# Two weight pairs of gate and up taken straight in each FFN instead of three

## The chip, the cores and the metric

The kernel runs on one core of a Trainium2 chip. The metric is the device time of one execution in microseconds (us), lower is better. The core has five engines with their own instruction queues: TensorE (PE in the profile, with its weight loads as PEld), VectorE (DVE), ScalarE (ACT), GpSimd (POOL) and SyncE (SP), which here only issues loads. Each executes its own queue in order and waits on semaphores for the others.

## The reference

A trunk of two layers over 512 tokens of width 1024. Each layer is a half-step FFN, a mixer (neighbourhood attention beside gated linear attention) and a second half-step FFN; a last norm follows. The change is in the FFN, which runs four times:

```python
D_MODEL = 1024; SEQ = 512; DEPTH = 2; D_FF = 2816

def rmsnorm(x, g):
    y = x * lax.rsqrt(jnp.mean(x * x, axis=-1, keepdims=True) + EPS)
    return y * g

def swiglu(h, w_gate, w_up, w_down):
    return (jax.nn.silu(h @ w_gate) * (h @ w_up)) @ w_down

# in hybrid_layer, twice per layer, with the mixer between:
x = x + 0.5 * swiglu(rmsnorm(x, ffn1_norm), ffn1_wg, ffn1_wu, ffn1_wd)
x = x + concat(neighbourhood attention, gated linear attention) @ w_out
x = x + 0.5 * swiglu(rmsnorm(x, ffn2_norm), ffn2_wg, ffn2_wu, ffn2_wd)
```

## The kernel before

The activations lie transposed, eight chunks of 128 features by 512 tokens (`xt`). Every fp32 operand is split into a high and a low half: ScalarE makes the high one by a copy (`split`, L149), VectorE the low one by a subtraction (L150), and each product is three matmuls, high x high, high x low, low x high (`mm3`, L169 to L171). So every matrix costs work on all three engines.

The 2816 hidden columns of gate and up are cut into 11 pairs of 2 x 128 columns, and the pairs into groups of 4, 4 and 3 (`GROUPS`); after each group its part of the down matrix follows (`down`), delayed into the next group's first pair. A pair's gate matrix and up matrix (1024 x 256 each, 1 MB) are multiplied in one of two ways.

- Straight (`direct_pairs`, `dmat`): from `XD`, the split of raw x times the norm's gain. It needs no norm factor; that is multiplied in afterwards (`evac`, L392 to L395). Two outputs by 8 chunks by 3 are 48 matmuls of 512 columns for a matrix. The weights come in four loads of 256 KB on ScalarE's queue (`dload`).
- By the block product (`smat`, `gate_up`): the weights and the normalised x are cut 2 x 2 and multiplied with seven products instead of eight. 7 x 4 x 3 are 84 matmuls of 256 columns for a matrix. The weights come in one 1 MB load on SyncE's queue; VectorE forms four sums of weight blocks (L269 to L272) and ScalarE and VectorE split seven blocks. The right-hand side is `XC`, which `prep_pair` makes from `xt` and the norm factor, two chunks at a time in four calls (L179 to L187 on VectorE, then its splits). All pairs of the FFN use the same `XC`.

At the start of an FFN the norm factor of a row (`stage_row`) is not there yet: the squares were summed while the last chunks of x were made, one matmul with ones adds them over partitions (L232), and ScalarE and VectorE take the inverse root (L242 to L250). The straight pairs stand in the first group, so that TensorE has work meanwhile: pair 0 (results in PSUM tiles `F_mm`), pair 1 (gate in `F_sc`, up in `F_tp` and `F_o`), pair 2 (`F_mm` again). `prep_pair` for chunks 0 to 5 is written between pair 1's gate and up matrices, that for the last two after the evacuation of pair 0; pairs 1 and 2 are evacuated after that. The block product then begins with pair 3.

The order of instructions on each engine isn't the order of the program text: a scheduler arranges them by its own cost estimates, over buffers of a fixed number (`wh` and `wl` six each, four PSUM tiles `mm`, two `sc`, one `tp` and `o`, five for the weight sums). It is fixed before the kernel runs. In the names of tiles, `F_xd` (`I_xd`, `OP_xd` in the first FFN and behind a mixer) are parts of `XD`, `F_xc` of `XC`, `F_y` its unsplit chunks, `F_wh` and `F_wl` the halves of a weight block, `F_wraw` a load, `F_ws` the weight sums, `F_r` the norm factor, `F_hid` the split hidden activations and `F_o` an evacuated result, or the PSUM tile "o".

Of the kernel before, what the change touches and what calls it, by code (L numbers as in the profile page):

```python
# [53 lines left out]
COLS = {"q": 0, "k": 512, "v": 1024, "gq": 1536, "gk": 1792, "gv": 2048, "gr": 2560}  # L54
TAGS = {'sl': 12, 'g0': 8, 'g1': 8, 'na': 6, 'ws': 5}
NPR = 12
NDF = 3
OPT = 2.56
OUTT = 8.24
GOTT = ('g0', 'g1')  # L60
# [3 lines left out]
def trunk_kernel(ctx, tc, xin, wgu, wdn, win, wcode, wgate, wout, vec, rpbt,  # L64
# [111 lines left out]
    def prep_pair(i, stage):  # L176
        s = st["s"]
        ya, yb = sl("y"), sl("y")
        V.scalar_tensor_tensor(ya, xt[:, 2 * i, :], gvec(stage, 2 * i), s, ALU.mult, ALU.mult)  # L179
        V.scalar_tensor_tensor(yb, xt[:, 2 * i + 1, :], gvec(stage, 2 * i + 1), s, ALU.mult, ALU.mult)  # L180
        ta, tb = sl("y"), sl("y")
        b11, b12, b21, b22 = ya[:, :H2], ya[:, H2:], yb[:, :H2], yb[:, H2:]
        t1, t2, t3, t4 = ta[:, :H2], ta[:, H2:], tb[:, :H2], tb[:, H2:]
        V.tensor_tensor(t1, b12, b11, op=ALU.subtract)
        V.tensor_tensor(t2, b22, t1, op=ALU.subtract)
        V.tensor_tensor(t3, b22, b12, op=ALU.subtract)
        V.tensor_tensor(t4, b21, t2, op=ALU.subtract)  # L187
        tag = ("na", "na", "g0", "g1")[i]
        h0 = sl("xc", F32R, tag)
        split(b11, h0[:, :H2], h0[:, H2:])  # L190
        parts = [(h0[:, :H2], h0[:, H2:])]
        if i < 2:
            xg = gp_.tile([P, 4, T], F32R, tag="ga", name=nm("xc"))
        for j, src in enumerate((yb, ta, tb)):
            if i < 2 and j < 2:
                h, l = xg[:, 2 * j, :], xg[:, 2 * j + 1, :]
            else:
                h, l = sl("xc", F32R, tag), sl("xc", F32R, tag)
            split(src, h, l)
            parts += [(h[:, :H2], l[:, :H2]), (h[:, H2:], l[:, H2:])]  # L200
        XC[i] = dict(zip(("b11", "b21", "b22", "t1", "t2", "t3", "t4"), parts))
# [128 lines left out]
    def dmat(*args):  # L330
        pss = []
        run(dmat_steps(pss, *args))
        return pss
# [24 lines left out]
    def ffn(l, which):  # L358
# [3 lines left out]
        stage = 3 * l + 2 * which  # L362
        fp = [NDF]

# [21 lines left out]
        def direct_pairs(hid):  # L386

            def evac(bg, bu):
                r = st["s"]
                for ps, pu in zip(bg, bu):  # L390
                    g, u = sl("o1"), sl("o2")
                    V.tensor_tensor(g, ps, r, op=ALU.mult)  # L392
                    S.activation(g, g, AF.Silu)
                    V.tensor_tensor(u, pu, r, op=ALU.mult)
                    V.tensor_tensor(u, u, g, op=ALU.mult)  # L395
                    add_hid(hid, u)

            raw, ws = st.pop("dpre", (None, None))
            b00 = dmat(wgu[idx, 0, 0], ("mm", "mm"), raw, ws)
            if stage == 0:  # L400
                nc.scalar.dma_start(con, onesid)
                for c in range(KD):
                    square(c)
            stage_row()
            b01 = dmat(wgu[idx, 0, 1], ("mm", "mm"))
            b10 = dmat(wgu[idx, 1, 0], ("sc", "sc"))
            for i in range(3):
                prep_pair(i, stage)
            b11 = dmat(wgu[idx, 1, 1], ("tp", "o"))
            evac(b00, b01)  # L410
            prep_pair(3, stage)
            if NDF == 3:
                b20 = dmat(wgu[idx, 2, 0], ("mm", "mm"))
            evac(b10, b11)
            if NDF == 3:
                evac(b20, dmat(wgu[idx, 2, 1], ("mm", "mm")))
# [45 lines left out]
        for g, n in enumerate(GROUPS):  # L462
            hid = []
            if g == 0:
                direct_pairs(hid)
                n -= NDF
                if stage == 0:
# [683 lines left out]
```

## Time and profile before

| | |
|---|---|
| three runs | 1954.86, 1954.99, 1955.47 us |
| the profiled execution | 1957.23 us, of which the trace spans 1955.5 |
| mean granted TensorE clock | 0.991 |
| PE busy | 1924.7 us, 12490 instructions |
| DVE busy | 1416.9 us, 2705 instructions |
| ACT busy | 1020.1 us, 1959 instructions |

All times below are from the one profiled execution and count from the start of its span. An instruction's duration holds the time until its result is out; the next one of the same engine may start earlier, so what a run of instructions costs is read from start to start. Matmul ends are modelled and overlap: a 512-column matmul is shown with 0.39 us, and the next starts 0.23 after it. A value in brackets behind a row is the time for which the engine stood idle before it, and what ended that.

### The profile page before, as it was taken

The page shows a single profiled execution, that of the slowest core. Times are in us where ns is not written, and L with a number is a line of the kernel's source. Part 1 is how long each engine was busy: PE and PEld are TensorE (multiplying, and loading weights), DVE is VectorE, ACT ScalarE, POOL GpSimd, SP SyncE. Part 2 cuts the span into 40 slices and gives each one's busy share as a digit, 9 for nine tenths or more (in the row PEclk, how much of TensorE's full clock was granted, in tenths as well). Part 3 has the DMA queues.
Part 4 walks back from the last instruction along what each step waited for, and adds up shares of the span by engine and source line. Part 5 has one row for each costly group of instructions (what it writes and reads, how often), then busy time and mean ns, then how long its engine had stood idle before and what let it go on. Part 6 is the DMA issues. An engine that isn't in the chain of part 4 may idle for free.

```text
span 1955.5 us, 32220 instructions
## 1 busy us (share of the span) xinstructions
PE 1924.7 (98%) x12490; PEld 1687.4 (86%) x12490; DVE 1416.9 (72%) x2705; ACT 1020.1 (52%) x1959; POOL 17.4 (1%) x36
## 2 busy tenths in 40 slices
PE   8999999999998999999999999999999999999997
PEld 7889989888777898999889899988887778999896
DVE  6958768676558875967788596776764689679585
ACT  5535536465564553644555364455654655546364
POOL 0000000000000000000000000000000000000000
PEclk9999999999999999999999999999999899999999
DMA  4333223322202332332223333232221033233322
GB/s 154 112 108 108 89 106 124 110 67 98 66 31 85 102 108 89 106 108 103 83 98 106 108 109 107 88 119 96 96 86 55 21 120 107 89 107 109 108 76 76
DMA packets 58249, 187.78 MB, mean 96 GB/s; under 512 B 6640, under 2 KB 13296, under 8 KB 45808
## 3 DMA queue, kind: packets, MB, share of 16 engines
q1 hardware_dynamic: 29904, 132.07, 19.8%
q10 hardware_dynamic: 25632, 45.27, 7.0%
q0 software_dynamic: 2560, 8.39, 1.3%
q8 instruction: 98, 1.61, 0.3%
q14 instruction: 55, 0.45, 0.1%
HBM read 183.60 MB, written 2.10 MB: 95 GB/s over the span
## 4 chain that ended last, share of the span: by engine, by line
PE 97%; DVE 1%; DMA 1%; ACT 1%; issue 0%; DVEq 0%; ACTq 0%
PE F_mm L169 14%; PE F_mm L171 14%; PE F_mm L170 14%; PE F_sc L169 9%; PE F_sc L170 9%; PE F_sc L171 9%; PE M_mm L169 6%; PE M_mm L170 6%; PE M_mm L171 6%; PE M_o L887 1%; PE M_sc L630 1%; PE M_tp L876 1%; PE M_sc L853 1%; PE M_mm L773 1%; PE M_sc L715 1%; DMA wraw<-in_wgu 0%
## 5 line engine op out<-in xcount | busy, mean ns | idle before, releaser
L149 ACT ACTIVATE F_wh<-F_wraw 128x512 fp32r<-128x512 f32 (+1 forms) x472 | 289.5, 617 | 439.9 <-PE F_sc L170 238.8
L169 PE MATMUL F_mm<-F_xc,F_wh 128*128 128x256 f32 x1792 | 500.5, 282 | 1.3 <-ACT F_wh L149 1.3
L170 PE MATMUL F_mm<-F_xc,F_wh 128*128 128x256 f32 x1792 | 501.5, 282 | 0.0
L171 PE MATMUL F_mm<-F_xc,F_wl 128*128 128x256 f32 x1792 | 495.2, 282 | 0.0
L150 DVE TENSOR_TENSOR F_wl<-F_wraw,F_wh 128x512 fp32r<-128x512 f32 (+1 forms) x472 | 312.8, 668 | 151.9 <-ACT F_wh L149 143.4
L169 PEld LDWEIGHTS F_mm<-F_xc,F_wh 128*128 128x128 f32 x1792 | 339.3, 190 | 3.7 <-ACT F_wh L149 1.9
L170 PEld LDWEIGHTS F_mm<-F_xc,F_wh 128*128 128x128 f32 x1792 | 340.3, 190 | 1.9
L171 PEld LDWEIGHTS F_mm<-F_xc,F_wl 128*128 128x128 f32 x1792 | 335.8, 190 | 0.0
L169 PE MATMUL F_sc<-F_hid,F_wh 128*128 128x512 f32 (+1 forms) x716 | 275.6, 387 | 1.3 <-DVE xt L455 1.3
L170 PE MATMUL F_sc<-F_hid,F_wh 128*128 128x512 f32 (+1 forms) x716 | 276.6, 386 | 0.0
L171 PE MATMUL F_sc<-F_hid,F_wl 128*128 128x512 f32 (+1 forms) x716 | 276.4, 386 | 0.0
L149 ACT ACTIVATE F_wh<-F_ws 128x512 fp32r<-128x512 f32 x256 | 161.8, 632 | 170.0 <-PE F_mm L170 109.8
L150 DVE TENSOR_TENSOR F_wl<-F_ws,F_wh 128x512 fp32r<-128x512 f32 x256 | 174.8, 688 | 41.8 <-ACT F_wh L149 38.8
L169 PEld LDWEIGHTS F_sc<-F_hid,F_wh 128*128 128x128 f32 x716 | 134.6, 188 | 29.0 <-DVE xt L455 3.0
L171 PEld LDWEIGHTS F_sc<-F_hid,F_wl 128*128 128x128 f32 x716 | 134.5, 188 | 26.4
L170 PEld LDWEIGHTS F_sc<-F_hid,F_wh 128*128 128x128 f32 x716 | 134.6, 188 | 25.7
L455 DVE SCALAR_TENSOR_TENSOR xt<-F_sc,xt 128x512 f32<-128x512 f32 x94 | 65.0, 691 | 96.7 <-PE F_sc L171 96.1
L169 PE MATMUL M_mm<-F_xd,M_wh 128*128 128x512 f32 x304 | 122.1, 403 | 0.0
L171 PE MATMUL M_mm<-F_xd,M_wl 128*128 128x512 f32 x304 | 120.3, 397 | 0.0
L170 PE MATMUL M_mm<-F_xd,M_wh 128*128 128x512 f32 x304 | 119.9, 395 | 0.0
L150 DVE TENSOR_TENSOR M_wl<-M_wraw,M_wh 128x512 fp32r<-128x512 f32 (+1 forms) x112 | 73.4, 669 | 35.9 <-ACT M_wh L149 32.4
L149 ACT ACTIVATE M_wh<-M_wraw 128x512 fp32r<-128x512 f32 (+1 forms) x112 | 67.6, 614 | 46.8 <-PE M_mm L170 37.9
(325 smaller groups left out, 3153.0 us busy)
## 6 DMA issues: line engine op xcount, KB each, us to landing
F_wraw<-in_wgu SPq DMA_DIRECT2D x64, 1024.0 KB, 4.7
F_wraw<-in_wdn SPq DMA_DIRECT2D x32, 1024.0 KB, 4.9
M_wraw<-in_win ACTq DMA_DIRECT2D x88, 256.0 KB, 3.6
F_wraw<-in_wgu ACTq DMA_DIRECT2D x80, 256.0 KB, 3.8
F_wraw<-in_wdn SPq DMA_DIRECT2D x16, 768.0 KB, 4.3
M_pp<-in_rpbt POOLq DMA_DIRECT2D x32, 256.0 KB, 3.1
M_wraw<-in_wout SPq DMA_DIRECT2D x16, 256.0 KB, 2.7
xt<-in_xin SPq DMA_DIRECT2D x8, 256.0 KB, 5.2
```

The lines of the kernel that those rows point to most:

```text
L149: S.activation(h, src, AF.Copy)
L150: V.tensor_tensor(l, src, h.bitcast(F32), op=ALU.subtract)
L169: PE.matmul(ps, wh, rh, start=first, stop=False, skip_group_check=more)
L170: PE.matmul(ps, wh, rl, start=False, stop=False, skip_group_check=more)
L171: PE.matmul(ps, wl, rh, start=False, stop=last, skip_group_check=more)
L455: V.scalar_tensor_tensor(xt[:, c, :], pss[j], 0.5, xt[:, c, :], ALU.mult, ALU.add)
L630: PE.matmul(pss[hh][o:o + 64, (i // 2) * 64:(i // 2 + 1) * 64], *op(hh, i), start=True, stop=True)
L715: PE.matmul(pss[hh][:, j * 256:(j + 1) * 256], kk[rows[hh], s * P:(s + 1) * P], qq[rows[hh], o:o + 256], start=True, stop=True)
L773: PE.matmul(dst, vs(2 * half + j), fa[:, o:o + P], start=False, stop=(j == 1))
L853: PE.matmul(sco[hh][:, jj * 256:(jj + 1) * 256], q[rows[hh], j * P:(j + 1) * P], krhs, start=True, stop=True)
L876: PE.transpose(pt[:, i * P:(i + 1) * P], pp[:, i * P:(i + 1) * P], idn)
L887: PE.matmul(po[rows[hh], j * P:(j + 1) * P], v[:, rows[hh]], pps[hh][:, (jj * 2 + c) * P:(jj * 2 + c + 1) * P], start=(c == 0), stop=(c == 1))
```

## The change

One number is changed, that of the straight pairs:

```diff
 TAGS = {'sl': 12, 'g0': 8, 'g1': 8, 'na': 6, 'ws': 5}
 NPR = 12
-NDF = 3
+NDF = 2
 OPT = 2.56
```

With it the two `if NDF == 3` branches of `direct_pairs` fall away (`b20` and its up matrix, and their evacuation), the counter `fp` from which `gate_up` takes its pairs begins at 2, and the first group has two block pairs instead of one. Per FFN, TensorE's order has 96 matmuls of 512 columns fewer and 168 of 256 columns more; over the whole program VectorE has 72 instructions more and ScalarE 24, in which eight issues of loads fewer per FFN are counted. The scheduler makes a new order from this. Three places of it, all in the third FFN (layer 2, first half):

TensorE before, where the straight pair 1 ends (`F_tp`, `F_o`) and pair 2's gate matrix follows:

```order
L171 MATMUL F_tp_10480<-F_xd_10188,F_wl_10497 128x512
L169 MATMUL F_o_10481<-F_xd_10188,F_wh_10503 128x512
L170 MATMUL F_o_10481<-F_xd_10188,F_wh_10503 128x512
L171 MATMUL F_o_10481<-F_xd_10188,F_wl_10504 128x512
L169 MATMUL F_mm_10594<-F_xd_9959,F_wh_10596 128x512
L170 MATMUL F_mm_10594<-F_xd_9959,F_wh_10596 128x512
L171 MATMUL F_mm_10594<-F_xd_9959,F_wl_10597 128x512
L169 MATMUL F_mm_10595<-F_xd_9959,F_wh_10603 128x512
```

and now at the same place:

```order
L171 MATMUL F_tp_10720<-F_xd_10428,F_wl_10737 128x512
L169 MATMUL F_o_10721<-F_xd_10428,F_wh_10743 128x512
L170 MATMUL F_o_10721<-F_xd_10428,F_wh_10743 128x512
L171 MATMUL F_o_10721<-F_xd_10428,F_wl_10744 128x512
L169 MATMUL F_mm_10875<-F_xc_10659,F_wh_10849 128x256
L170 MATMUL F_mm_10875<-F_xc_10659,F_wh_10849 128x256
L169 MATMUL F_mm_10902<-F_xc_10656,F_wh_10857 128x256
L170 MATMUL F_mm_10902<-F_xc_10656,F_wh_10857 128x256
L171 MATMUL F_mm_10875<-F_xc_10659,F_wl_10850 128x256
```

What followed was 96 matmuls on `XD`; now the first matmul on `XC` is the next row. Fifty-five rows on, TensorE's order now has this piece, where the last parts of `XC` are read for the first time:

```order
L169 MATMUL F_mm_10875<-F_xc_10825,F_wh_10853 128x256
L170 MATMUL F_mm_10928<-F_xc_10822,F_wh_10869 128x256
L171 MATMUL F_mm_10928<-F_xc_10821,F_wl_10870 128x256
L170 MATMUL F_mm_10875<-F_xc_10826,F_wh_10853 128x256
L171 MATMUL F_mm_10875<-F_xc_10825,F_wl_10854 128x256
L169 MATMUL F_mm_10996<-F_xc_10664,F_wh_10974 128x256
L170 MATMUL F_mm_10996<-F_xc_10665,F_wh_10974 128x256
L169 MATMUL F_mm_11023<-F_xc_10656,F_wh_10978 128x256
```

The last of these rows is the 63rd matmul of the block product in the order. `F_xc_10826` is the low half of a part of the last chunk pair, and the last of all to be made. VectorE's order before, around the split that makes it (there `F_xc_10586`):

```order
L150 TENSOR_TENSOR F_wl_10693<-F_wraw_10678,F_wh_10692 128x512
L187 TENSOR_TENSOR F_y_10569<-F_y_10565,F_y_10568 128x256
L150 TENSOR_TENSOR F_xc_10582<-F_y_10568,F_xc_10581 128x512
L395 TENSOR_TENSOR F_o_1965_10661<-F_o_1965_10661,F_o_1964_10660 128x512
L395 TENSOR_TENSOR F_o_1968_10670<-F_o_1968_10670,F_o_1967_10669 128x512
L150 TENSOR_TENSOR F_xc_10586<-F_y_10569,F_xc_10585 128x512
```

and now:

```order
L150 TENSOR_TENSOR F_wl_10924<-F_ws_10863,F_wh_10923 128x512
L187 TENSOR_TENSOR F_y_10809<-F_y_10805,F_y_10808 128x256
L150 TENSOR_TENSOR F_wl_10971<-F_wraw_10968,F_wh_10970 128x512
L270 TENSOR_TENSOR F_ws_10983<-F_ws_10982,F_wraw_10968 128x512
L150 TENSOR_TENSOR F_xc_10822<-F_y_10808,F_xc_10821 128x512
L395 TENSOR_TENSOR F_o_1998_10830<-F_o_1998_10830,F_o_1997_10829 128x512
L395 TENSOR_TENSOR F_o_2001_10839<-F_o_2001_10839,F_o_2000_10838 128x512
L150 TENSOR_TENSOR F_xc_10826<-F_y_10809,F_xc_10825 128x512
```

From the first instruction on the finished norm factor (L179) to this split VectorE's order had 66 rows (8 of L179 and L180, 20 of 256 columns, 38 of 512), and has 74 now (8, 20, 46): sums and splits for the first block product have come in between. In the fourth FFN it is the same count, in the second 8, 20 and 50, in the first 8, 20 and 52.

## Rows read from the trace of the kernel before

**Rows 1.** the page's totals: busy us, share, instructions; then the chain
```profile
PE 1924.7 (98%) x12490; PEld 1687.4 (86%) x12490; DVE 1416.9 (72%) x2705; ACT 1020.1 (52%) x1959; POOL 17.4 (1%) x36
...
PE 97%; DVE 1%; DMA 1%; ACT 1%; issue 0%; DVEq 0%; ACTq 0%
```

**Rows 2.** waits of PE: engine, line <- releaser: us, times, longest
```profile
PE M_mm L169 <- ACT M_on L777: 6.0, 2, 3.0
PE F_mm L169 <- ACT I_wh L149: 4.2, 2, 3.9
...
PE F_mm L169 <- ACT F_wh L149: 1.3, 3, 0.4
```

**Rows 3.** windows of DVE, FFN 3: stretch, us, busy (instructions), PEclk, DMA, GB/s
```profile
995.50:1030.50 35.00, 34.97 (x67) 1.00 0.27 92
1030.50:1046.00 15.50, 8.88 (x15) 1.00 0.20 68
```

**Rows 4.** timeline of DVE, third FFN
```profile
995.59 0.75 DVE L179 SCALAR_TENSOR_TENSOR F_y<-xt,vecs,F_r 128x512 f32<-128x512 f32 x1
...
996.92 0.42 DVE L184 TENSOR_TENSOR F_y<-F_y 128x256 f32<-128x256 f32 x1
997.25 0.42 DVE L150 TENSOR_TENSOR F_xc<-F_y,F_xc 128x256 fp32r<-128x256 f32 x1
...
1021.37 0.68 DVE L150 TENSOR_TENSOR F_hid<-F_o,F_hid 128x512 fp32r<-128x512 f32 x1
...
1022.57 0.68 DVE L150 TENSOR_TENSOR F_wl<-F_wraw,F_wh 128x512 fp32r<-128x512 f32 x1
...
1029.85 0.68 DVE L150 TENSOR_TENSOR F_xc<-F_y,F_xc 128x512 fp32r<-128x512 f32 x1
```

**Rows 5.** timeline of PE, pair 1 to pair 2, FFN 3: start, us, instruction
```profile
1002.57 0.39 PE L169 MATMUL F_sc<-F_xd,F_wh 128*128 128x512 f32 x1
...
1024.33 0.39 PE L169 MATMUL F_mm<-F_xd,F_wh 128*128 128x512 f32 x1
```

**Rows 6.** timeline of PE, block product's matmuls, second FFN
```profile
698.76 0.28 PE L169 MATMUL F_mm<-F_xc,F_wh 128*128 128x256 f32 x1
...
704.61 0.28 PE L170 MATMUL F_mm<-F_xc,F_wh 128*128 128x256 f32 x1
```

**Rows 7.** timeline of DVE, first rows after the norm, other FFNs
```profile
35.16 0.68 DVE L150 TENSOR_TENSOR F_wl<-F_wraw,F_wh 128x512 fp32r<-128x512 f32 x1
...
648.25 0.75 DVE L179 SCALAR_TENSOR_TENSOR F_y<-xt,vecs,F_r 128x512 f32<-128x512 f32 x1
...
1611.57 0.75 DVE L179 SCALAR_TENSOR_TENSOR F_y<-xt,vecs,F_r 128x512 f32<-128x512 f32 x1
```

**Rows 8.** timeline of PE, pair 1's first matmul, other FFNs
```profile
35.62 0.39 PE L169 MATMUL F_sc<-I_xd,F_wh 128*128 128x512 f32 x1
...
655.24 0.39 PE L169 MATMUL F_sc<-OP_xd,F_wh 128*128 128x512 f32 x1
...
1618.25 0.39 PE L169 MATMUL F_sc<-OP_xd,F_wh 128*128 128x512 f32 x1
```

**Rows 9.** timeline of ACT, third FFN
```profile
1031.15 0.63 ACT L149 ACTIVATE F_wh<-F_wraw 128x512 fp32r<-128x512 f32 x1 [2.35 <-PE F_mm L170]
...
1049.63 0.37 ACT L290 ACTIVATE F_o<-F_mm 128x256 f32<-128x256 f32 x1
1049.89 0.38 ACT L291 ACTIVATE F_o<-F_mm 128x256 f32<-128x256 f32 x1
```

**Rows 10.** the page's DMA issues: KB each, us to landing
```profile
F_wraw<-in_wgu SPq DMA_DIRECT2D x64, 1024.0 KB, 4.7
```

**Rows 11.** timeline of PE after its wait in the mixer
```profile
590.41 0.50 PE L169 MATMUL M_mm<-M_oh,M_wh 128*128 128x512 f32 x1 [3.02 <-ACT M_on L777]
```

**Rows 12.** windows of PE: stretch, us, busy (matmuls), PEclk, DMA, GB/s
```profile
13.00:18.20 5.20, 5.01 (x12) 0.50 0.57 190
...
591.00:596.00 5.00, 5.00 (x16) 0.66 0.00 0
```

## The prediction

> **What bounds the kernel now.** I read the page's totals first, then its chain that ended last. TensorE is busy 1924.7 of 1955.5 us, and 97% of the chain is its own work; VectorE has 72% and ScalarE 52% [rows 1]. Then TensorE's waits over the whole run: the longest belong to the mixer and to the very first load, and inside the FFNs, where the change is, only three short ones stand, 1.3 us together, where the block product takes over from the straight pairs [rows 2]. So each matmul taken away is worth its pitch, as long as nothing else becomes late. Whether something does is not seen in shares, which are averages; it is seen in VectorE's own timeline around that handover, in the third FFN (layer 2, first half). From the first row after the row norm, at 995.59, to 1030.50 VectorE is busy 34.97 of 35.00 us; in the 15.5 us after that, 8.88 [rows 3]. The split that is its last work for the block product's right-hand side (`F_xc<-F_y`) starts at 1029.85, at the end of that full stretch [rows 4]. The average of 72% hides one stretch per FFN in which VectorE has no slack at all, and it lies just ahead of the place that the change touches.
>
> **What the change does to TensorE.** Per FFN a straight pair goes: 2 matrices of 48 matmuls of 512 columns. From 1002.57 to 1024.33 there are 96 of them, 0.2267 us each [rows 5], so 21.76 us. A block pair comes: 2 x 84 matmuls of 256 columns. From 698.76 to 704.61 there are 49 steps, 0.1194 us each [rows 6], so 20.06 us. The difference is 1.70 us per FFN, 6.8 us over four. That is all the change can give.
>
> The Trainium skill ("TensorE: Matmul & The Clock Gate", section "Wait — 56ns, not 53.3ns?") has N divided by 2.4 GHz plus about 2.5 ns as the warm start-to-start time: 215.8 and 109.2 ns. By that, an estimate, the exchange would give 2.37 us per FFN, 9.5 in all; the rows show 0.2267 and 0.1194, so they don't agree with it to the nanosecond, and the rows decide.
>
> **What it does to VectorE.** A straight pair costs VectorE 8 splits of weights, 6 products of the evacuation and 2 splits of `hid`: 16 instructions of 512 columns at 0.60 us (1021.37 to 1022.57 is two steps [rows 4]), 9.6 us for 21.8 us of matmuls. A block pair has 34: four sums, seven splits of weights and four narrow additions per matrix, then two products and two splits of `hid`: 26 x 0.60 + 8 x 0.336 = 18.3 us for 20.06 us of matmuls. So VectorE's work grows by 8.7 us per FFN. What decides is where that falls, and what cover is lost. In the kernel before, the third pair's 21.8 us of matmuls need only raw x, so they run while VectorE still makes the eight XC tiles, evacuates pairs 0 and 1 and splits weights. That pair is gone, and behind pair 1's last straight matmul TensorE's row order has the block product at once.
>
> I therefore walk VectorE's order of the changed kernel with prices of rows before. Prices: 0.665 us for the two scaled products (995.59 to 996.92 is two), 0.33 to 0.34 for 256 columns (996.92 to 997.25; I use 0.336), 0.60 for 512 [rows 4]. A test of the walk on the kernel before: its order has 8 + 20 + 38 instructions of the three kinds from the first after the row norm to the last XC split, 5.3 + 6.7 + 22.8 = 34.84; from 995.59 that ends at 1030.43, and the trace has 1029.85 + 0.60 = 1030.45 [rows 4]. In the changed order the stretch in the same FFN holds 8 + 20 + 46, since weight sums and splits for the first block product now stand between: 39.64 us. In FFN 4 it is the same, in FFN 2 it is 8 + 20 + 50, in FFN 1 it is 8 + 20 + 52 (42.04 and 43.24 us). The starting points are 35.16, 648.25, 995.59 and 1611.57 [rows 4, 7]; a result is there 0.08 after its step. So the last split is ready at 78.5, 690.4, 1035.3 and 1651.3.
>
> TensorE's side: it starts pair 1's gate matrix at 35.62, 655.24, 1002.57 and 1618.25 [rows 5, 8]. With 96 straight matmuls (21.76) and 62 block matmuls that stand ahead of the last held row (7.40) it would arrive at 64.8, 684.4, 1031.7 and 1647.4. In FFN 3 and 4 a further chain hangs on that split, since the next product of the row order needs a PSUM buffer that is released behind it: one matmul 0.28 [rows 6], a ScalarE copy ahead in its queue 0.63, the two evacuations, 0.26 to the second and 0.38 in it [rows 9]: 1.55 us. The waits are then 13.7, 6.0, 5.1 and 5.4 us, 30.2 together. FFN 1 is the worst because there VectorE gets the row norm only 0.5 us before TensorE begins pair 1 (35.16 against 35.62), in the others 6.7 to 7.0 us before.
>
> Bounds of this term: below, 13.7 us, if only the first FFN waits; above, some 40 us, if each of the 306 instructions of the four stretches loses 0.03 us to waits for ScalarE's halves of the splits, of which the full stretch before shows nearly none (0.03 us idle in 35.00 [rows 3]). I take the value in between that the walk gives, since the walk hit the row of before to 0.02 us.
>
> **Loads and ScalarE.** Eight 256 KB loads on ScalarE's queue go and two 1 MB loads on SyncE's queue come in per FFN, the bytes being the same; a 1 MB load lands 4.7 us after its issue [rows 10], so one issued a pair ahead, with 20 us of matmuls before it is needed, comes in time. ScalarE gets 14 more instructions and 8 issues fewer per FFN; it has 48% of the span free [rows 1], and in the full stretch VectorE hardly waits for it [rows 3]. I take both at 0, with 0 to 2 us per FFN should the first 1 MB load of the first FFN be late (its buffer comes free only a few us before it is needed). Behind the handover the block pairs need 18.3 us of VectorE per 20.06 of TensorE, so the gap doesn't widen again; the mixers keep their order nearly and get 0, give or take 2 us.
>
> **The clock.** A waiting TensorE may lose more than the wait. After a wait of 3.02 us in the mixer, ended at 590.41 [rows 11], the granted clock falls to 0.66 over 591 to 596: the lower level (1.2 GHz) for two thirds of it, a loss of 5.0 x 0.34 = 1.7 us; in the opening, after a wait for loads, 5.2 us run at 0.50, a loss of 2.6 [rows 12]. In the new waits TensorE works in between, so I take three losses of 1.7 over the four FFNs, 5 us (the first FFN first of all), with bounds of none and two in each FFN, 13.6.
>
> **The sum.** 1957.23 (the profiled execution) + 30.2 waits − 1.3 waits of before that they replace − 6.8 for the exchange + 5 clock = 1984.3. The profiled execution stands 2.2 us above the median of the runs, 1954.99; on that scale it is 1982.1. I predict 1982 us, 27 us or 1.4% slower.
>
> **The rivals.**
> A second theory is that the clock or the lag costs much more: VectorE, once late, feeds the block product piece by piece, and TensorE falls to half speed twice in every FFN. Waits as above and 13.6 for the clock: 1957.23 − 2.2 + 22.1 + 13.6 = 1991. For it speaks that after a single 3 us wait the clock fell [rows 12]; against it, that the matmuls come in groups between the waits, and that the new waits aren't all as long. A rule in the Trainium skill (the same page, section "HAM oscillation — how this bites in real kernels") speaks for this one: waits for data between bursts of matmuls bring the slow clock back each time. The 0.66 agrees in kind; the number above does not hang on it.
>
> A third: only the first FFN waits, since in the others VectorE's 7 us of head start are used better than I think (XC first, evacuation behind). 13.7 + 1.7 − 1.3 − 6.8 = 7.3: 1962. Against it: rows on VectorE go in the order written for it, and that order has the evacuations ahead of the last XC split in all four.
>
> The other side: VectorE keeps up, and the 1.70 us per FFN stays as gain. The place is the same handover, the mechanism VectorE's pace while ScalarE and the loads press less on it: the point from which it decides is 0.60 us per instruction of 512 columns falling to about 0.48 in FFN 2 to 4 (5 to 6 us over 46 to 50 of them is 0.11 to 0.12) and 0.34 in the first (13.7 over 52). Then 1955.0 − 6.8 = 1948, and with part of the first FFN's wait left, up to 1955. No row shows such a pace at 512 columns, for which 256 columns take 0.33 [rows 4].
>
> **How the numbers follow.** My forecast gets 0.70, with its own range 1972 to 1990; the clock rival 0.13, the first-FFN-only one 0.09, the other side 0.08, of which 0.05 for a real gain and 0.03 for no change. A measurement of this kernel tells 0.2%, 3.9 us, from no change. The range 1968 to 1993 takes in nearly all of the forecast and most of the clock rival, and leaves out the other two. Slower by over 0.2% is 0.70 + 0.13 + 0.09 = 0.92, faster 0.05, same 0.03.
>
> **What would show it.** In the changed kernel's trace TensorE waits at the start of the block product in every FFN, for VectorE's `F_xc` or `F_wl` splits and for what ScalarE makes behind them, about 14 us in the first and 5 to 6 in the others; VectorE has no idle time from the row norm to the last XC split, and that split ends near 78.5 in the first FFN. TensorE's chain loses about 6.8 us of matmuls, the granted clock is under 1 just behind the waits, and mixers take what they took. I am wrong if those waits are absent or if most of the added time stands in the mixers or in waits for loads.

## The result, and the profile after

The changed kernel took 1978.14 us (median of four runs, 1976.77 to 1980.02), the kernel before 1954.92 on the same chip: 1.0124 times, 95% interval 1.0109 to 1.0139. The forecast was 1982 us, with a range of 1968 to 1993. The profiled execution took 1978.77 us, with a span of 1977.0 against 1955.5.

The totals and the chain of the page after, to be laid beside [rows 1]:

```profile
PE 1926.0 (97%) x12778; PEld 1700.8 (86%) x12778; DVE 1453.0 (73%) x2777; ACT 1044.5 (53%) x2015; POOL 17.4 (1%) x36
...
PE 92%; DVE 5%; ACT 1%; DMA 1%; issue 1%; DVEq 0%; ACTq 0%
```

TensorE's busy time rose by 1.3 us only, though the straight pairs that went are dearer than the block pairs that came. Its waits over the whole run, largest of the FFNs and, for size, the mixer's own (us in total, times, longest):

```profile
PE F_mm L170 <- DVE F_xc L150: 8.8, 5, 3.4
PE F_mm L171 <- DVE F_wl L150: 8.3, 5, 2.4
PE M_mm L169 <- ACT M_on L777: 6.0, 2, 3.0
...
PE F_mm L169 <- ACT F_o L291: 2.6, 2, 1.3
PE F_mm L169 <- ACT F_wh L149: 1.7, 3, 0.7
...
PE F_mm L169 <- ACT F_xc L149: 0.8, 1, 0.8
```

Where there were three short waits of 1.3 us in the FFNs [rows 2], there are now 8.8 for VectorE's `F_xc`, 8.3 for its `F_wl`, and 5.1 for what ScalarE makes behind them. The mixer's 6.0 is as it was. The chain gives VectorE 5% where it had 1. All the new waits stand within some 20 us behind the handover: 8.9 us in the first FFN, 4.3, 4.3 and 4.8 in the others, 22.4 in all.

VectorE in the four stretches from the norm factor to the last split of `XC` (window, us, busy us and instructions):

```profile
34.60:77.00 42.40, 42.40 (x81) 0.87 0.23 80
655.70:696.70 41.00, 40.97 (x78) 0.96 0.22 77
1008.60:1048.30 39.70, 39.69 (x75) 0.96 0.23 80
1627.20:1667.00 39.80, 39.77 (x76) 1.00 0.23 81
```

It is busy all the time in each, as it was in the one stretch of [rows 3]. The third FFN's last norm step and its last split of `XC`:

```profile
1007.89 0.69 DVE L250 SCALAR_TENSOR_TENSOR F_r<-F_a,F_r 128x512 f32<-128x512 f32 x1
...
1047.68 0.70 DVE L150 TENSOR_TENSOR F_xc<-F_y,F_xc 128x512 fp32r<-128x512 f32 x1
```

The distance is 39.79 us. The first instruction behind the norm step starts 0.72 us after it, at 1008.61; from there the walk in the prediction gives 39.64 up to the end of the split's turn, less its 0.60: 39.76 in all. In the first FFN it is 42.34:

```profile
33.98 0.69 DVE L250 SCALAR_TENSOR_TENSOR F_r<-F_a,F_r 128x512 f32<-128x512 f32 x1
...
76.32 0.70 DVE L150 TENSOR_TENSOR F_xc<-F_y,F_xc 128x512 fp32r<-128x512 f32 x1
```

TensorE in the third FFN: the start of pair 1, two places in the wait, and the row at which it goes on for good:

```profile
1014.89 0.39 PE L169 MATMUL F_sc<-F_xd,F_wh 128*128 128x512 f32 x1
...
1045.43 0.58 PE L171 MATMUL F_mm<-F_xc,F_wl 128*128 128x256 f32 x1 [2.38 <-DVE F_wl L150]
...
1048.44 0.51 PE L170 MATMUL F_mm<-F_xc,F_wh 128*128 128x256 f32 x1
...
1050.60 0.39 PE L169 MATMUL F_mm<-F_xc,F_wh 128*128 128x256 f32 x1 [1.30 <-ACT F_o L291]
```

and the evacuation in ScalarE that releases it:

```profile
1050.17 0.37 ACT L291 ACTIVATE F_o<-F_mm 128x256 f32<-128x256 f32 x1
```

TensorE began pair 1 at 1014.89. The 96 straight matmuls and the 62 block matmuls ahead of its held row, at the prediction's pitches 29.16 us, would have brought it there at 1044.05. It went on at 1050.60, after the last split (1047.68 + 0.70), the copies ahead in ScalarE's queue and the PSUM evacuation L291: 6.5 us later. Between, it worked for a while at 0.21 us per matmul, 0.41 us shown for one, where [rows 6] have 0.12 and 0.28. That is the clock. The granted clock behind the handover of the four FFNs (window, us, busy us and matmuls, then the clock):

```profile
60.00:66.00 6.00, 1.48 (x6) 0.97 0.13 41
66.00:72.00 6.00, 3.35 (x14) 0.50 0.00 0
72.00:78.00 6.00, 4.26 (x18) 0.50 0.00 0
78.00:84.00 6.00, 6.00 (x48) 0.89 0.53 175
694.00:700.00 6.00, 3.95 (x15) 0.50 0.01 3
...
1046.00:1051.00 5.00, 3.70 (x20) 0.73 0.00 0
...
1670.00:1675.00 5.00, 5.00 (x32) 0.66 0.54 185
```

In the first FFN TensorE is held from 60 us on, and 12 us run at 0.50, the lower level of 1.2 GHz; the other FFNs have one stretch each.

Where the time went, by segments of the two timelines. An FFN is counted from the row norm's matmul (L232) to the next stage's first matmul. For the third FFN these are, before and after,

```profile
990.81 0.59 PE L232 MATMUL F_tp<-F_acc,con 128*128 128x512 f32 x1
...
1315.01 0.39 PE L169 MATMUL M_mm<-F_xd,F_wh 128*128 128x512 f32 x1
```

```profile
1003.13 0.59 PE L232 MATMUL F_tp<-F_acc,con 128*128 128x512 f32 x1
...
1331.55 0.39 PE L169 MATMUL M_mm<-F_xd,F_wh 128*128 128x512 f32 x1
```

324.20 and 328.42 us. All of them, and the same segments of the experiments that matter below (the fourth FFN to the last matmul):

| us | FFN 1 | FFN 2 | FFN 3 | FFN 4 | sum | against before |
|---|---|---|---|---|---|---|
| before | 317.4 | 324.2 | 324.2 | 339.3 | 1305.1 | |
| changed | 329.2 | 328.8 | 328.4 | 345.3 | 1331.8 | +26.7 |
| filler (fill24) | 330.4 | 328.2 | 328.2 | 344.4 | 1331.1 | +26.0 |
| low halves left out (lowcut) | 324.6 | 323.2 | 323.5 | 339.4 | 1310.6 | +5.5 |
| four straight pairs (ndf4) | 318.5 | 325.3 | 325.3 | 341.0 | 1310.0 | +4.9 |
| xc_first | 323.8 | 325.9 | 325.9 | 342.1 | 1317.6 | +12.5 |
| xc_prio_only | 327.5 | 325.4 | 327.4 | 341.6 | 1321.8 | +16.7 |

The rest of the span, mixers and opening, gave 5.1 us back. No mixer code changed; its segments differ by some us between all these kernels (the stretch from the first mixer's first matmul to the next row norm is 295.4 us before, 291.9 after, 291.3 with the filler). The granted clock goes with it. Here are TensorE's windows around the places of the two mixers where it is under 1, before and then after (window, us, busy us and matmuls, then the clock):

```profile
550.00:640.00 90.00, 82.41 (x426) 0.92 0.20 65
1515.00:1565.00 50.00, 45.56 (x303) 0.90 0.08 25
```

```profile
560.00:610.00 50.00, 45.56 (x302) 0.90 0.07 22
1530.00:1580.00 50.00, 45.57 (x310) 0.93 0.10 32
```

In the opening, from 10 to 30 us, it is 0.83 before and 0.91 after. If TensorE works all through, these stretches lose 15.6 us of clock before and 10.3 after, 5.3 less. That is the size of the 5.1, though it does not come out segment by segment. Why the slow stretches come and go with the scheduler's order was not tested.

### The profile page after: what moved, and what is told of

Same layout as the page of the kernel before. It is cut to its first block, busy times and chain, and to the rows that moved or that the text cites. A ratio compares the mean times of both kernels' runs of the same rounds, so it can differ in the third digit from the quotient of the medians.

```text
span 1977.0 us, 32927 instructions
## 1 busy us (share of the span) xinstructions
PE 1926.0 (97%) x12778; PEld 1700.8 (86%) x12778; DVE 1453.0 (73%) x2777; ACT 1044.5 (53%) x2015; POOL 17.4 (1%) x36
## 4 chain that ended last, share of the span: by engine, by line
PE 92%; DVE 5%; ACT 1%; DMA 1%; issue 1%; DVEq 0%; ACTq 0%
PE F_mm L169 13%; PE F_mm L171 13%; PE F_mm L170 13%; PE F_sc L169 9%; PE F_sc L170 9%; PE F_sc L171 9%; PE M_mm L169 6%; PE M_mm L170 6%; PE M_mm L171 6%; PE M_o L887 1%; PE M_sc L630 1%; DVE F_wl L150 1%; PE M_tp L876 1%; PE M_sc L853 1%; DVE F_xc L150 1%; PE M_sc L715 1%
## 5 line engine op out<-in xcount | busy, mean ns | idle before, releaser
L170 PE MATMUL F_mm<-F_xc,F_wh 128*128 128x256 f32 x2016 | 568.4, 284 | 8.8 <-DVE F_xc L150 8.8
L169 PE MATMUL F_mm<-F_xc,F_wh 128*128 128x256 f32 x2016 | 566.5, 284 | 5.2 <-ACT F_o L291 2.6
L171 PE MATMUL F_mm<-F_xc,F_wl 128*128 128x256 f32 x2016 | 562.4, 284 | 8.3 <-DVE F_wl L150 8.3
L149 ACT ACTIVATE F_wh<-F_wraw 128x512 fp32r<-128x512 f32 (+1 forms) x464 | 284.5, 616 | 406.5 <-PE F_sc L170 239.1
L150 DVE TENSOR_TENSOR F_wl<-F_wraw,F_wh 128x512 fp32r<-128x512 f32 (+1 forms) x464 | 308.3, 670 | 140.7 <-ACT F_wh L149 137.6
L170 PEld LDWEIGHTS F_mm<-F_xc,F_wh 128*128 128x128 f32 x2016 | 386.5, 192 | 12.1 <-DVE F_xc L150 10.3
L169 PEld LDWEIGHTS F_mm<-F_xc,F_wh 128*128 128x128 f32 x2016 | 385.1, 192 | 8.5 <-ACT F_o L291 3.0
L171 PEld LDWEIGHTS F_mm<-F_xc,F_wl 128*128 128x128 f32 x2016 | 382.1, 192 | 9.6 <-DVE F_wl L150 9.5
L149 ACT ACTIVATE F_wh<-F_ws 128x512 fp32r<-128x512 f32 x288 | 182.1, 632 | 186.8 <-PE F_mm L170 114.1
L150 DVE TENSOR_TENSOR F_wl<-F_ws,F_wh 128x512 fp32r<-128x512 f32 x288 | 197.0, 690 | 42.3 <-ACT F_wh L149 39.0
```

The costliest lines, as they stand in the source:

```text
L149: S.activation(h, src, AF.Copy)
L150: V.tensor_tensor(l, src, h.bitcast(F32), op=ALU.subtract)
L169: PE.matmul(ps, wh, rh, start=first, stop=False, skip_group_check=more)
L170: PE.matmul(ps, wh, rl, start=False, stop=False, skip_group_check=more)
L171: PE.matmul(ps, wl, rh, start=False, stop=last, skip_group_check=more)
```

## The experiments

Theory one is the prediction's: VectorE's work up to the last split of `XC` sets when TensorE goes on. The rival is that something else holds TensorE, a load, a buffer, or ScalarE.

**Work put into the wait (fill24).**

```diff
             b11 = dmat(wgu[idx, 1, 1], ("tp", "o"))
             evac(b00, b01)
+            pf, (xh, _) = psum("mm"), XD[KD - 1]
+            for i in range(24):
+                PE.matmul(pf, xh[:, :P], xh, start=i == 0, stop=i == 23)
```

> The changed kernel with 24 matmuls of 512 columns more per FFN, put between the last straight matmul and the block product; they read one split chunk of x, their result is thrown away, and VectorE and ScalarE get nothing from them. They are 24 x 0.2267 = 5.4 us of TensorE's time per FFN, 21.8 us over four. Theory one (TensorE waits there for VectorE's last split of XC, so work put in the wait is free): FFN 2 to 4 lose 6.4 to 7.6 us each to the wait and the slow clock behind it, FFN 1 loses 13.9, so the 5.4 us fit in everywhere and the time is 1972 to 1980 us, the longest waits shrinking by 5.4 us. Theory two (TensorE is held by something that moves along with it, a load, a PSUM buffer or ScalarE's evacuations behind its own matmuls): the filler comes on top, 1978 + 22 = 2000 us.

Measured: 1980.34 us (1978.72 to 1982.22), +2.2 us on the changed kernel for 21.8 us of added matmuls. The FFN segments together are 0.7 us shorter than without them. TensorE's waits around the handover of the third FFN, all that the view gives:

```profile
PE F_mm L169 <- ACT F_o L291: 0.4, 1, 0.4
```

and of the first:

```profile
PE F_mm L170 <- DVE F_xc L150: 2.8, 1, 2.8
PE F_mm L171 <- DVE F_wl L150: 2.0, 1, 2.0
```

The 5.4 us went into the wait and emptied it in FFN 2 to 4; in the first 4.8 of 8.9 us are left. VectorE's order up to the last split is nearly the same as without the filler, 79, 73, 73 and 73 instructions instead of 79, 76, 74 and 74. This decides against a rival that moves along with TensorE, such as evacuations behind its own matmuls; something that is late at a fixed time, such as a load, is not excluded by it.

**VectorE's work taken away (lowcut).**

```diff
     def wsplit(src, n=T):
+        if st.get("cut"):
+            h = wp.tile([P, T], F32R, tag="wh", name=nm("wh"), bufs=6)
+            S.activation(h[:, :n], src[:, :n], AF.Copy)
+            return h, h
...
+            st["cut"] = n == NDF
             yield from smat(wgu[idx, n, 0], post_g)
             yield from smat(wgu[idx, n, 1], post_u)
+            st["cut"] = False
```

> The changed kernel without VectorE's subtraction for the weights of the first block pair of every FFN: the high half stands in for the low one, so that pair's products lose their low weight half (the output is not the reference's there). Loads, ScalarE's copies and all matmuls stay as many. VectorE's order up to the last split of XC has 71, 69, 69 and 69 instructions instead of 79, 76, 74 and 74, that is 4.8, 4.2, 3.0 and 3.0 us less at 0.60 each. Theory one (VectorE's last split of XC sets when TensorE goes on): the waits shrink by just that, 15 us over four FFNs, and some 3 to 6 us of slow clock go with them: 1957 to 1963 us. Theory two (loads, ScalarE or buffers hold TensorE, VectorE being late only beside them): 1976 to 1980 us.

Measured: 1958.20 us (ten runs, 1952.44 to 1963.83), 20 us less with the same loads, ScalarE instructions and matmuls. (The high half goes in twice.) The waits left behind the handover in the third FFN, of 4.3 us in the changed kernel:

```profile
PE F_mm L173 <- ACT F_o L295: 0.5, 1, 0.5
PE F_mm L173 <- ACT F_wh L166: 0.4, 1, 0.4
```

In the first FFN 5.4 of 8.9 us are left. Theory one again, and with the same loads that rival falls too. The low halves left out are also tiles that TensorE waits for (`F_wl`), so the run shows that it is VectorE's amount of work; which of its results is the late one it doesn't tell. That a free buffer let VectorE go on is unlikely, since in the changed kernel it had no gap in this stretch.

**The exchange by itself (ndf4).**

```diff
-NDF = 2
+NDF = 4
...
+            if NDF == 4:
+                b30 = dmat(wgu[idx, 3, 0], ("sc", "sc"))
+                evac(b30, dmat(wgu[idx, 3, 1], ("tp", "o")))
```

> Four straight pairs per FFN instead of three: the same edit in the other direction. Theory one (a straight pair costs TensorE 1.70 us more than a block pair and nothing else changes, as VectorE has the whole first group as cover): the kernel before + 6.8 - up to 1.3 for its short waits at the handover, 1960.4 to 1961.7 us. Theory two (the two ways of taking a pair cost TensorE the same, and the exchange is worth nothing in itself): 1954 to 1955 us. Theory three (the difference is 2.37 us per FFN, from the published start-to-start times): 1963 to 1964.5 us.

Measured: 1956.55 us (1952.65 to 1960.85), 1.0012 times before, interval 1.0000 to 1.0023: by the whole time between theories one and two, since opening and mixers took 6.6 us less here. By the segments: 1.0, 1.1, 1.1 and 1.8 us more per FFN, and the three waits of 0.43 us, one in each of the first three, are gone, so the exchange is worth 1.43, 1.50, 1.48 and 1.75 us per FFN, 6.2 in all, not the 6.8 of the prediction nor 9.5.

**Another order (xc_first, xc_prio_only).** The first has all of this. The second has the preparation's part alone: the higher priority, and the last `prep_pair` ahead of pair 0's evacuation:

```diff
+DEFER = 7
...
-            for i in range(3):
-                prep_pair(i, stage)
+            with tc.high_priority(offset=400):
+                for i in range(3):
+                    prep_pair(i, stage)
             b11 = dmat(wgu[idx, 1, 1], ("tp", "o"))
+            with tc.high_priority(offset=400):
+                prep_pair(3, stage)
             evac(b00, b01)
-            prep_pair(3, stage)
...
-            evac(b10, b11)
+            late.append(lambda: evac(b10, b11))
...
                 gu = gate_up(hid)
+                if late:
+                    for _ in range(DEFER):
+                        next(gu)
+                    late.pop()()
```

> The changed kernel with two moves on VectorE and ScalarE: the four preparations of XC get a higher priority in the scheduler, and the evacuation of straight pair 1 is written into the first block pair, after its gate matrix's products. The same instructions on every engine, another order: up to the last split of XC VectorE has 70, 63, 63 and 63 instructions instead of 79, 76, 74 and 74, that is 37.2 us in FFN 1 and 33.0 us in the others. TensorE would come to the held row 29.7 us after that start in FFN 1 and 36.1 in the others. Theory one (the last split of XC sets when TensorE goes on): no wait in FFN 2 to 4, which then take 1.7 us less than before the change, some 21 us less than now, and about 5 us less in FFN 1: 1949 to 1954 us. Theory two (VectorE has too much work in that stretch in whatever order, and the wait moves to weight splits further on): 1965 to 1978 us.

Measured: 1967.26 us (1965.76 to 1969.66). 10.9 us were won, not 24 to 29. FFN 1 did as theory one had it, 5.4 us less. In FFN 2 to 4 TensorE no longer waits for `XC`, but the segments stay 1.7 to 2.8 us above before instead of going 1.7 below: there are other waits now. TensorE's, around the handover of the third FFN:

```profile
PE F_mm L170 <- ACT F_o L292: 1.4, 1, 1.4
PE F_mm L170 <- ACT F_wh L150: 0.9, 2, 0.5
PE F_mm L170 <- ACT F_o L301: 0.7, 1, 0.7
```

and what ScalarE does before the longest of them (in brackets the idle time and what ended it):

```profile
1034.49 1.15 ACT L150 ACTIVATE F_wh<-F_wraw 128x512 fp32r<-128x512 f32 x2 [1.12 <-PE F_mm L171]
1035.55 0.36 ACT L291 ACTIVATE F_o<-F_mm 128x256 f32<-128x256 f32 x1
1035.81 0.38 ACT L292 ACTIVATE F_o<-F_mm 128x256 f32<-128x256 f32 x1
```

ScalarE stood idle for a weight buffer that TensorE had to free, and the evacuation TensorE waits for was queued behind two weight splits. The number fits theory two, its cause does not: it is ScalarE's queue and not VectorE that is late next.

> The changed kernel with the higher priority for the preparation of XC alone; the evacuation of pair 1 stays where it was. Up to the last split of XC VectorE has 74, 67, 67 and 67 instructions, 39.6 us in FFN 1 and 35.4 in the others, against 42.6, 40.8, 39.6 and 39.6 in the changed kernel and 37.2, 33.0, 33.0 and 33.0 with the later evacuation as well. Theory one (the time of the last split is all that counts as long as it is late): FFN 1 gains 3 us and loses less to the slow clock, FFN 2 to 4 come to their held row in 36.1 us and find the split just made: 1962 to 1968 us, a little above or level with the run that has both moves (1967). Theory two (the later evacuation gave most of that run's gain): 1972 us or more.

Measured: 1967.27 us (1965.52 to 1969.53), level with both moves together, so by the median the preparation's part gave all of the gain. By the segments of the profiled executions (1969.53 us here, 1966.73 with both) the later evacuation is worth another 3.7 us in FFN 1 and 1.5 in FFN 3, and costs 0.5 in each of the other two; the medians don't show that.

**The first FFN kept (mix3222).** `NDF = (3, 2, 2, 2)`, one number for each FFN.

> Three straight pairs in the first FFN, two in the other three. Theory one (the loss of each FFN is its own: 11.8 us in the first, whose VectorE gets the row norm only as TensorE begins pair 1, and 4.2 to 6.0 in each of the others): the changed kernel - 11.8 = 1966 us, give or take 3 us by which the mixers differ from run to run of the scheduler. Theory two (what FFN 1 loses is won back further on, or the losses add up over the FFNs): 1972 us or more.

Measured: 1971.59 us (1969.78 to 1972.66), at the edge between the two. FFN 1's segment is 317.5 us, as before the change, so its 11.8 us are its own. But FFN 3 and 4 took 1.8 and 1.2 us more than in the changed kernel and the second mixer with its output 3.4, with the slow clock at other places.

**Sums on GpSimd (pool_sums, xc_first_pool, mix_xc_first_pool).** `st["pool"]` is set for the first block pair of an FFN.

```diff
+        E = G if st.get("pool") else V
-        V.tensor_tensor(s1, a21, a22, op=ALU.add)
+        E.tensor_tensor(s1, a21, a22, op=ALU.add)
...
```

> The changed kernel with the eight sums of weight blocks of each FFN's first block pair on GpSimd instead of VectorE; the same sums, nothing left out. Up to the last split of XC VectorE has 71, 69, 69 and 69 instructions instead of 79, 76, 74 and 74, as in the run without the low weight halves. Theory one (only the number of VectorE's instructions counts): 1957 to 1963 us as there. Theory two (GpSimd takes much longer for a sum than VectorE, so splits of the sums come late, or VectorE's pace of 0.60 us rises while GpSimd works): 1968 to 1990 us, with TensorE's waits at the products on weight sums instead of at XC.

> XC's preparation first and the evacuation of pair 1 later, as in the run before of that kind, and the sums of the first block pair on GpSimd as well. VectorE has 62, 56, 56 and 56 instructions up to the last split of XC, 32.4 us in FFN 1 and 28.8 in the others; TensorE would come there after 29.7 and 36.1. Theory one: no wait for XC in FFN 2 to 4, some 3 us in FFN 1; what is left there are short waits for ScalarE: 1951 to 1959 us. Theory two (GpSimd's sums are late): 1965 us or more, waits at the products on weight sums.

> The same with three straight pairs in the first FFN, where VectorE has the least head start. Theory one: 1.5 us of exchange gained in each of three FFNs less short waits for ScalarE of up to 3 us each, FFN 1 as before the change: 1950 to 1957 us, not clearly faster than before. Theory two (GpSimd's sums are late): 1960 us or more.

Measured: 1986.65 us, 8.5 more than the changed kernel; 1968.83 with XC first, 1.6 more than without GpSimd; 1961.67 with three pairs in the first FFN. By the time that is theory two in all three. But TensorE's longest waits in the first of them are still those for `XC`:

```profile
PE F_mm L170 <- DVE F_xc L150: 9.5, 6, 4.8
...
PE F_mm L171 <- DVE F_wl L150: 4.2, 4, 1.3
```

GpSimd's sums in its third FFN, and VectorE beside them:

```profile
1026.78 2.09 POOL L270 TENSOR_TENSOR F_ws<-F_wraw 128x512 f32<-128x512 f32 x1 [323.11 <-DVE F_o L397]
1028.95 1.63 POOL L271 TENSOR_TENSOR F_ws<-F_ws,F_wraw 128x512 f32<-128x512 f32 x1
1030.66 1.62 POOL L272 TENSOR_TENSOR F_ws<-F_wraw,F_ws 128x512 f32<-128x512 f32 x1
```

```profile
1027.63 0.69 DVE L395 TENSOR_TENSOR F_o<-F_mm,F_r 128x512 f32<-128x512 f32 x1
1028.23 1.19 DVE L150 TENSOR_TENSOR F_wl<-F_wraw,F_wh 128x512 fp32r<-128x512 f32 x1
1029.35 0.68 DVE L397 TENSOR_TENSOR F_o<-F_mm,F_r 128x512 f32<-128x512 f32 x1
1029.95 1.18 DVE L150 TENSOR_TENSOR F_wl<-F_wraw,F_wh 128x512 fp32r<-128x512 f32 x1
1031.06 1.78 DVE L179 SCALAR_TENSOR_TENSOR F_y<-xt,vecs,F_r 128x512 f32<-128x512 f32 x1
```

A sum that takes VectorE 0.69 us takes GpSimd 1.6 to 2.1 here, and 1.3 to 8.0 over the run. And VectorE's own splits with two operands in SBUF take 1.18 and 1.19 us here, a scaled product 1.78, where [rows 4] have 0.68 and 0.75; those that read one operand from PSUM (L395, L397) stay at 0.68 and 0.69. Not each instruction with two SBUF operands is slowed: a split at 1026.69, as GpSimd's first sum begins, took 0.69, and that sum 2.09. The Trainium skill ("SBUF — State Buffer", section "SBUF: two separate sides") has VectorE's instructions with two SBUF inputs and GpSimd's share one pair of ports, held for a whole instruction; these rows agree. So VectorE has 69 instructions instead of 74 up to the last split in this FFN, and takes 40.27 us from the first to that split's start instead of 39.07: theory two by VectorE's pace, with the longest waits still at `XC`.

**Combinations (mix_xc_first, mix_xc_first_wh7, before_wh7).** The first joins mix3222 and xc_first (FFN 1 with its evacuation where it was); the other two get one buffer more for the high halves of weights, the last with three straight pairs everywhere:

```diff
-        return [wp.tile([P, T], F32R, tag=t, name=nm(t), bufs=6) for t in ("wh", "wl")]
+        return [wp.tile([P, T], F32R, tag=t, name=nm(t), bufs=7 if t == "wh" else 6) for t in ("wh", "wl")]
```

> Three straight pairs in the first FFN, two in the others, XC's preparation first and the evacuation of pair 1 later in those; no GpSimd. By the segments measured so far: FFN 1 as before the change, FFN 2 and 3 1.7 us and FFN 4 2.8 us above before (1.5 gained by the exchange, 3 to 4 lost in short waits for ScalarE's splits and evacuations behind the handover): 1955 + 6 = 1961 us, give or take 3 us from the mixers.

Measured: 1954.60 us (ten runs, 1951.78 to 1960.48; before 1956.10 on the same chip), 0.9997 times before, interval 0.9985 to 1.0009: no difference. Below what was expected; the segments of its profile (execution of 1957.77 us) are near it, +4.8 us in the FFNs for 6.2, and the mixers again take less.

> The same with seven buffers for the high halves of weights instead of six. In the run with XC first ScalarE stood idle at the handover until TensorE freed such a buffer (1.86 and 1.12 us), and its evacuations of PSUM are queued behind that split. Theory one (that buffer is what holds ScalarE): the waits of 0.5, 1.4, 0.4 and 0.7 us per FFN shrink to under 1 us together, 1952 to 1956 us. Theory two (VectorE's low halves, or their buffers, of which there are still six, hold it as well, and VectorE's new order has 67 instructions up to the last split again): 1959 to 1964 us, no change.

Measured: 1951.95 us, 0.9980 times before, interval 0.9970 to 0.9990. That is theory one's time, but not its cause. Its waits should have shrunk to under 1 us per FFN; in the trace FFN 2 to 4 have 2.9, 2.6 and 2.8 us behind the handover, where mix_xc_first has 2.9, 3.0 and 2.9, for VectorE's `F_wl` and ScalarE's evacuations now. What did change is the mean granted clock, 0.994 instead of 0.992, some 4 us over the span.

> The kernel before the change, three straight pairs, with seven buffers for the high halves of weights. Theory one: its three waits of 0.43 us at the handover, for ScalarE's split that waits for such a buffer, go: 1953 to 1955 us. Theory two (the scheduler's new order brings other waits): up to 1958 us.

Measured: 1947.01 us (seven runs, 1945.04 to 1948.40), 0.9957 times before, interval 0.9944 to 0.9969, below both theories. It is the fastest kernel here, ahead of the kernel before and of all with two straight pairs. The page's totals and, from TensorE's waits, those that stand where the three for `F_wh` at the handover are gone:

```profile
PE 1918.2 (99%) x12490; PEld 1682.6 (86%) x12490; DVE 1409.1 (72%) x2705; ACT 1014.2 (52%) x1959; POOL 17.4 (1%) x36
```

```profile
PE F_mm L169 <- ACT F_o L300: 0.9, 2, 0.5
```

So 1.3 us of waits went and 0.9 came, 0.4 of the 9 us. The mean granted clock is 0.995 instead of 0.991, some 8 us over the span, and TensorE is busy 6.5 us less for the same 12490 matmuls: most of the gain is less time at the lower clock. Why the new order has fewer such stretches was not taken apart.

## Why the prediction was right, and where its steps were off

The cause and the place. TensorE waits behind the handover in all four FFNs, VectorE has no gap up to the last split, and FFN 1 is the worst. fill24 and lowcut show the cause, one by filling the wait and one by shortening VectorE's work; ndf4 shows that the exchange itself is a gain, as forecast.

The walk. Its 39.76 us for the stretch in FFN 3 met 39.79. For FFN 1 and 2 the count under "The change", which the walk took over, was one and two instructions too high (51, one of them of 384 columns, and 48 of 512 in the order, not 52 and 50), so the last split came 0.9 and 1.2 us earlier than walked.

The wait and the clock. Forecast: 30.2 us of waits and 5 of clock behind them, 35.2. Measured as lost: the segments' changes, plus the exchange from ndf4, plus 0.43 for the wait of before in FFN 1 to 3, that is 13.6, 6.6, 6.1 and 7.8 us, 34.1 in all. The prediction's waits are a lag, the time by which TensorE comes late past its held row, and its clock term is what is lost behind that row. Counted so, at the prediction's pitches, TensorE passes the held rows (at 77.19, 698.02, 1050.60 and 1669.16) 13.3, 6.4, 6.5 and 5.7 us late, 32.0 in all, and loses another 3.8 behind them, at the lower clock. Both terms were met within 2 us. (Their sum, 35.8, is 1.7 above the 34.1, in part since the exchange was worth less than those pitches say.) One of the four was luck: in FFN 2 the last split came 1.2 us earlier than walked, and a weight split behind it (`F_wl`) held TensorE 1.0 us more, which the walk did not have.

What was wrong is what the lag is made of. Idle time is 22.4 us, and most of the other 11.7 are matmuls at the lower clock. Most of these run while VectorE is late in any case; they take the place of idle time and cost nothing more. Only what is still slow after the last result is there comes on top, as at 1670 to 1675. The forecast that the waits view would show 14, 6, 5 and 5.5 us was wrong for that reason, 8.9, 4.3, 4.3 and 4.8 being there.

The exchange. 1.70 us per FFN was mis-sized: 1.43 to 1.50 came in the first three and 1.75 in the fourth, in ndf4's step from three pairs to four. The pitches were taken inside unbroken runs of one kind; what is lost where the two kinds meet or the order is mixed isn't in them. Which of these it is stays open.

The mixers. They were costed at 0, give or take 2, and this term failed: they and the opening gave 5.1 us back, with less time at the lower clock. This is most of why the time is 1978 and not 1982: the profiled executions differ by 26.7 − 5.1 = 21.6 us, and for the FFNs 27.1 had been forecast. The medians differ by 23.2, since the profiled execution before was 2.3 us above its median and the one after 0.6. That they differ by such amounts in every kernel measured, without a change in them, sets what a time of this kernel can tell: a single FFN's change is better read from its segment.

The rivals. The clock rival fell: the lower clock was there for longer than the forecast had it, but mostly inside the wait, and behind it 3.8 us came and not 13.6. The first-FFN-only one fell: 15 of the 26.7 us are from the other three (and mix3222 keeps them). The other side fell: VectorE's pace was 0.60 us as before.

## What to carry to other kernels

An engine that is busy 72% of the span may be the bound of one stretch: before work is taken away from the bounding engine, ask what the others finish beneath it, and walk their order to the point where they must be done. Filler that costs no other engine anything, put in a suspected wait, tells in one run whether the wait is a shadow of another engine's work. And when a wait on one engine is cleared, look at once at the queue of the next, here ScalarE's. One weight buffer more made the kernel before 0.4% faster, more than the change could have given at its best, but its trace has the gain in the granted clock and not in the waits that the buffer was meant for: a time that fits a theory doesn't show the theory's cause, so look for the waits it names.

## What was not expected of the hardware

While TensorE waited piece by piece in the first FFN, the granted clock was 0.50 for 12 us, with 3.35 and 4.26 us of work in the two windows of 6 us, so much of a wait can be filled with slow matmuls. GpSimd's elementwise work slowed some of VectorE's instructions on two SBUF operands, splits from 0.68 to 1.19 us and scaled products from 0.75 to 1.78, and left those with a PSUM operand at 0.68 and 0.69. In the mixers the stretches at the lower clock came and went with the order of the FFNs, though no mixer code changed: 90 us at 0.92 and 50 at 0.90 before, 50 at 0.90 and 50 at 0.93 after.
